# One PSUM bank moved from transposes to products in a two-layer decoder step, and output rows that begin in the heads' banks

## The chip, the cores and the metric

The kernel runs on one core of a Trainium2 chip. The metric is device time in microseconds (us), lower is better. The figures of before are the median of three runs and one execution taken by the hardware profiler. TensorE is called PE, VectorE DVE, ScalarE ACT, GpSimd POOL and SyncE SP, as in the profile.

## The reference

One inference step of a decoder trunk with two layers, for a prompt of 512 tokens and for 8 samples of 4 new tokens each, with the same weights. The change touches only the second layer (mixer B), from the attention over the shared latent cache to the final norm. Cut to that:

```
# MLA: q_lat, q_rope from a low-rank query; c_kv (256) and k_rope (64) shared by 8 heads
s = (einsum('bthc,bsc->bhts', q_lat, ckv) + einsum('bthr,bsr->bhts', q_rope, krope)) * MLA_SCALE
p = softmax(where(kpos <= qpos, s, -1e30))
o_lat = einsum('bhts,bsc->bthc', p, ckv)
tok = einsum('bthc,chd->bthd', o_lat, w_v_up)            # 8 heads x 128
mixed = concatenate([tok * silu(gate_t), mem_o * silu(gate_m)])   # 1024 + 512 wide
x = x + mixed @ w_out[l]                                  # 1536 x 1024
y = rmsnorm(x, g_final)
```

The prompt attends to its own 512 tokens. Each sample attends to 4096 cached tokens, which lie in 32 pages of 128 found through a page table, and to its own 4. `mem_o` is attention into 256 memory tokens. All data are float32.

## The kernel before, in words

Products that need float32 accuracy are made of three matmuls in a faster format: `split` (L88 to L91) makes a rounded high part (ACT, L89) and the remainder (L90, on DVE or on POOL, by its last argument), and `mm3` (L93 to L96) multiplies high by high, high by low and low by high. `transpose` (L135) is a matmul with the identity.

Up to about 478 us the kernel computes layer A, the shared keys and most gates. From L942 on the instruction order of PE and of SP (which issues most loads) is the order of the program text, while the other engines' instructions are ordered by the compiler's own scheduler. The program text is written by a planner: each piece of work is a generator (`Thread`, L947) that emits some instructions and then yields a pair, the PE time they are taken to need and the time until its next piece is due (both in us), or a condition. `weave` (L957) always continues the due thread that is least far along (`base + span * spent / work`). The planner knows nothing of PSUM banks, so a change of banks alone does not change the order.

The threads after 478 us:

- `round_scores` (rs) and `round_values` (rv): the samples' attention over the cache in 16 rounds. A round loads two halves of 8 pages (`load_half`, L998, into buffers `a` and `b`; a load is issued when the value matmuls of an earlier round have freed the buffer), transposes part of the keys (`turn_keys`, L1027; bank `tr`, copied out to `kt` by ACT L1019 or DVE L1021), multiplies queries by keys (L1051, L1060; bank `ac`), takes the softmax (L1069, L1071), transposes the weights (bank `tr`, copied out to `rt` by DVE L1083) and multiplies by the values (L1088; bank `ac`).
- `gates_late` (gl), then `head_inputs` (hi): queries, keys and values of the prompt's heads. Their products lie in bank `pa` and are read out by DVE L1227 (queries) or by a split (L89, L90 to `kx`, `vx`).
- `heads` (ha): per head, four blocks of scores (two banks `hs`), mask and softmax (L1280 to L1286, the last being the scaling of `e` by DVE), then per block transposes into `hs` (`turn_weights`), a split to `p`, and value products into bank `po`, read out by DVE L1320.
- `own_scores` (os_): the samples' scores against their own four tokens, in bank `tr`.
- `out_all` (out): the output projection in two column halves `fh` of 512. Each half has four row blocks of 128 tokens and six slabs of `w_out` (256 rows x 512 columns, tile `wr`, split into `wh` and `wl`). Slabs are made by `prepare` (L1359), three of them ahead of the output. Row blocks accumulate in four banks `oa` over all slabs; slab 4 is done together with slab 5, and `done` (L1400) adds the residual, sums squares and, in the second half, scales and stores.
- `sample_out` (so): `combine` puts the samples' partial attentions together through a chain of transposes and products in bank `tr`, and then six pairs of slabs (tile `ws`, five buffers, loaded again as PE frees them) give the samples' output rows in bank `ac` (L1622).

The order of the threads: rv, rs and gl until gl is done; rv, rs, ha and hi until all heads have their scores; rv, rs, ha and os_ until these are done; then the heads' banks are closed and four `oa` banks opened; at last so and out. The eight PSUM banks, each 128 x 512 float32, are shared out like this:

```
    rb = Banks(tr=2, ac=2)
    hb = Banks(pa=1, po=1, hs=2)
```

`ps_(tag)` gives the next bank of a tag; with one bank it waits for the last reader of the tile ahead.

Of the kernel before, what the change touches and what calls it, by code (L numbers as in the profile page):

```python
# [8 lines left out]
F32R = mybir.dt.float32r  # L9
# [6 lines left out]
P = 128  # L16
# [22 lines left out]
def trunk_kernel(ctx: ExitStack, tc: tile.TileContext, A, O):  # L39
    nc = tc.nc  # L40
# [47 lines left out]
    def split(h, l, src, eng=None):  # L88
        nc.scalar.copy(h, src)  # L89
        (eng or nc.vector).tensor_tensor(out=l, in0=src, in1=fr(h), op=ALU.subtract)  # L90
        return h, l  # L91
# [21 lines left out]
    ps_ = Banks(pa=4, tr=3, ac=1)  # L113
# [411 lines left out]
    t, v = load_w(wa[22], KD, P)  # L525
# [207 lines left out]
    for j in range(4):  # L733
        t = xo("o")
# [222 lines left out]
    def weave(threads, last):  # L957

        through = last if callable(last) else lambda: all(t.done for t in last)
        while not through():  # L960
            can = [
                t
                for t in threads
                if not t.done and t.at <= now[0] and (t.until is None or t.until())
            ]
            if not can:
                now[0] += 0.1
                assert now[0] < 2000
                continue
            t = min(can, key=Thread.behind)  # L970
            t.until = None
            got = next(t.gen, None)
            if got is None:
                t.done = True
            elif callable(got):
                t.until = got
            else:
                now[0] += got[0]
                t.spent += got[0]
                t.at = now[0] + got[1]  # L980


    rb = Banks(tr=2, ac=2)
    hb = Banks(pa=1, po=1, hs=2)

    def ps_(tag):
        return (rb if tag in rb.tags else hb)(tag)
# [361 lines left out]
    slabs = [(fh, s) for fh in range(2) for s in range(6)]  # L1349
    order = ([0, 1], [2, 3], [4, 5], [8, 9], [10, 11], [6, 7])  # L1350

    def slab(t, fh, s):
        k = order[s][0]
        v = t.rearrange("p (k c) -> p k c", k=2)
        src = wo[k * P : (k + 2) * P, fh * 512 : (fh + 1) * 512]
        nc.sync.dma_start(v, src.rearrange("(k p) c -> p k c", p=P))
        return v

    def prepare(fh, s):  # L1359
        if fh == 0:  # L1360
            for k in order[s]:
                mix_b(k)
        t = fin("wr")
        slab(t, fh, s)
        wh, wl = split(fin("wh", F32R), fin("wl", F32R), t, nc.gpsimd)
        return wh.rearrange("p (k c) -> p k c", k=2), wl.rearrange("p (k c) -> p k c", k=2)

    prepared = [prepare(*slabs.pop(0)) for _ in range(3)]
# [15 lines left out]
        gains_f.extend([gfin, gfs])  # L1384

    def out_rows(fh):
        pts = [ps_("oa") for _ in range(4)]

        pieces = [[(pts[j], 0, 512)] for j in (0, 3, 1, 2)]
        if fh:  # L1390
            pieces[3] = [(pts[2], 0, 256), (ps_("ac"), 256, 256)]

        def run(s, j, piece, wh, wl):
            ps, o, n = piece
            c, w = slice(j * P, (j + 1) * P), slice(o, o + n)
            for i, k in enumerate(order[s]):
                h, l = mixed[k]
                mm3(ps[:, :n], h[:, c], l[:, c], wh[:, i, w], wl[:, i, w], s == 0 and i == 0, s == 5 and i == 1)

        def done(j, p, ps, o, n):  # L1400
            f = slice(fh * 512 + o, fh * 512 + o + n)
            xf = x1n[j][:, f]
            nc.vector.tensor_tensor(out=xf, in0=ps[:, :n], in1=xf, op=ALU.add)
            c = 4 * j + 2 * fh + p
            nc.scalar.activation(pat("wu", n=n), xf, AF.Square, scale=D ** -0.5, accum_out=ssq[:, c : c + 1])
            if fh == 0:
                nc.vector.tensor_tensor(out=xf, in0=xf, in1=gains_f[0][:, f], op=ALU.mult)
                return
            if p < len(pieces[j]) - 1:
                return  # L1410
            sm = st(3)
            others = [4 * j] + [4 * j + 2 + i for i in range(p)]
            so_far = EPS
            for i, o_ in enumerate(others):
                nc.vector.tensor_scalar(
                    out=sm[:, i : i + 1], in0=ssq[:, o_ : o_ + 1], scalar1=so_far, scalar2=None, op0=ALU.add
                )
                so_far = sm[:, i : i + 1]
            r = st(1)
            nc.vector.tensor_scalar(  # L1420
                out=sm[:, 2:3], in0=ssq[:, c : c + 1], scalar1=so_far, scalar2=None, op0=ALU.add
            )
            nc.gpsimd.tensor_tensor(out=r, in0=sm[:, 2:3], in1=mhalf[:, :1], op=ALU.pow)
            nc.scalar.activation(x1n[j][:, :512], x1n[j][:, :512], AF.Copy, scale=r)
            nc.sync.dma_start(O["y_p"][0, j * P : (j + 1) * P, :512], x1n[j][:, :512])
            xf = x1n[j][:, 512:]
            nc.vector.scalar_tensor_tensor(out=xf, in0=xf, scalar=r, in1=gains_f[0][:, 512:], op0=ALU.mult, op1=ALU.mult)
            nc.sync.dma_start(O["y_p"][0, j * P : (j + 1) * P, 512:], xf)

        late = []  # L1430
        for s in range(6):
            wh, wl = prepared.pop(0)
            late.append((s, wh, wl))
            if s == 4:
                continue
            for j in range(4):
                for p, piece in enumerate(pieces[j]):
                    for one in late:
                        run(one[0], j, piece, *one[1:])
                        yield 1.4 / len(pieces[j]), 0.0  # L1440
                    if s == 5:
                        if not x1n:
                            yield lambda: x1n
                        done(j, p, *piece)
            for _ in late:
                if slabs:
                    prepared.append(prepare(*slabs.pop(0)))
            late = []

    def out_all():  # L1450
        yield from out_rows(0)
        yield from out_rows(1)
# [29 lines left out]
        yield 0.5, 0.0  # L1482

    os_ = Thread(own_scores(), 1.0, 0.0, 1.0, now[0])
    weave([rv, rs, ha, os_], [ha, os_])
    hb.close()
    hb = Banks(oa=4)
    out = Thread(out_all(), 112 / total, 66 / total, 66.0, now[0])
    weave([rv, rs, out], [rv, rs])
    sp_order.__exit__(None, None, None)  # L1490
    nats.close()
# [113 lines left out]
    def sample_out():  # L1605
        todo = [(fh, s) for fh in range(2) for s in range(6)]
        o = cb("o").rearrange("p (b c) -> p b c", b=NB - 1)
        nc.sync.dma_start(o, ostore.rearrange("b p c -> p b c"))
        parts.update({b: o[:, b, :] for b in range(NB - 1)})
        v = [pat("vx") for k in range(2)]  # L1610
        for k in range(2):
            src = A["w_v_up"][k * P : (k + 1) * P].rearrange("p h c -> p (h c)")
            nc.sync.dma_start(v[k], src)
        here = [slab(cb("ws"), *todo.pop(0)) for _ in range(5)]
        yield from combine(cb, v)
        for fh in range(2):
            psm = ps_("ac")
            for s, ks in enumerate(order):
                v = here.pop(0)
                for i, k in enumerate(ks):  # L1620
                    for j in range(4):
                        nc.tensor.matmul(  # L1622
                            psm[j * NS : (j + 1) * NS, :P],
                            lhsT=gs[:, k, :],
                            rhs=v[:, i, j * P : (j + 1) * P],
                            start=s == 0 and i == 0,
                            stop=s == 5 and i == 1,
                        )
                if todo:
                    here.append(slab(cb("ws"), *todo.pop(0)))  # L1630
                if s % 2:
                    yield 0.88, 0.5
            fs = slice(fh * P, (fh + 1) * P)
            nc.vector.tensor_tensor(out=x1s[:, fs], in0=psm[:, :P], in1=x1s[:, fs], op=ALU.add)
            nc.scalar.activation(pat("wu")[:, :P], x1s[:, fs], AF.Square, accum_out=sss[:, fh : fh + 1])
        sq = st(1)
        nc.vector.tensor_tensor(out=sq, in0=sss[:, 0:1], in1=sss[:, 1:2], op=ALU.add)
        yield 0.0, 1.5
        po = ps_("tr")
        nc.tensor.matmul(po[:, 0:1], lhsT=jsum, rhs=sq, start=True, stop=True)  # L1640
        r = rstd_cols(po[:, 0:1], 1, P, D)
        nc.vector.scalar_tensor_tensor(out=x1s, in0=x1s, scalar=r, in1=gains_f[1], op0=ALU.mult, op1=ALU.mult)
        for j in range(4):
            nc.sync.dma_start(
                O["y_s"].rearrange("b t (f j c) -> j (b t) f c", f=2, j=4)[j],
                x1s[j * NS : (j + 1) * NS, :].rearrange("p (f c) -> p f c", f=2),
            )
# [134 lines left out]
```

## Time and profile before

| | us |
|---|---|
| median of 3 runs | 840.11 |
| lowest and highest run | 835.95, 843.13 |
| the profiled execution | 836.81 |
| its span, first to last instruction | 835.0 |
| PE busy in that span | 782.3 (94%) |
| DVE busy | 495.0 (59%) |
| ACT busy | 316.1 (38%) |
| POOL busy | 242.3 (29%) |

Busy times overlap between engines. A line of the profile names source line, engine, operation and tiles as out<-in without buffer numbers. A value in brackets behind an instruction is the idle time of its engine just ahead of it and what ended it. A table of stretches gives for each engine the busy time and in brackets the number of instructions. PE's clock is the share of full speed that was granted.

### The profile page before, as it was taken

The numbers are of one execution on the slowest core, as the hardware profiler recorded it, in microseconds if no ns is written. First come the engines' busy times: TensorE is split into PE (matmuls) and PEld (weight loads), VectorE is DVE, ScalarE is ACT, GpSimd is POOL, SyncE is SP. The second block draws the span as 40 slices with busy tenths as digits, with TensorE's granted clock in tenths as the row PEclk, the third lists the DMA queues.
The fourth block names the chain that finished last, engine by engine and source line by source line (L and its number), as shares of the span: only waits on it lengthen the run. The fifth ranks groups of instructions, "written<-read, shape, count | busy, mean of one in ns | idle before, by whom it ended". The sixth has DMA issues, their size and how long they took to land.

```text
span 835.0 us, 17362 instructions
## 1 busy us (share of the span) xinstructions
PE 782.3 (94%) x6814; PEld 669.6 (80%) x6814; DVE 495.0 (59%) x942; ACT 316.1 (38%) x631; POOL 242.3 (29%) x216
## 2 busy tenths in 40 slices
PE   6999999999999999889999999897999899979895
PEld 6989998999999989768998886675676667757584
DVE  6757666798834435965676545565566474673213
ACT  7453333432433234435343223434344443522212
POOL 0035220111243323404332435352142141054141
PEclk9999999999999999999999999999999999989998
DMA  8356247431233337347426698897897887778512
GB/s 308 93 182 222 75 177 263 148 89 52 77 95 95 85 118 222 123 137 237 164 69 248 217 388 310 316 360 255 312 362 260 299 322 270 249 271 291 204 55 101
DMA packets 83060, 169.54 MB, mean 203 GB/s; under 512 B 9377, under 2 KB 26402, under 8 KB 82722
## 3 DMA queue, kind: packets, MB, share of 16 engines
q1 hardware_dynamic: 77170, 149.61, 52.5%
q0 software_dynamic: 5808, 18.82, 6.1%
q8 instruction: 54, 0.88, 0.4%
q14 instruction: 28, 0.23, 0.1%
HBM read 157.19 MB, written 11.21 MB: 202 GB/s over the span
## 4 chain that ended last, share of the span: by engine, by line
PE 72%; DMA 10%; DVE 9%; ACT 4%; issue 2%; SPq 1%; POOL 1%; POOLq 0%; DVEq 0%; ACTq 0%
PE pa L94 15%; PE pa L96 14%; PE pa L95 14%; DMA b<-in_cache_P 4%; PE tr L135 4%; PE ac L1088 3%; PE ac L1051 3%; PE oa L94 2%; PE oa L96 2%; PE oa L95 2%; DMA ws<-in_w_out_b 2%; PE ac L1060 1%; PE ac L393 1%; DMA wr<-in_w_mem_v 1%; SPq L1010 1%
## 5 line engine op out<-in xcount | busy, mean ns | idle before, releaser
L94 PE MATMUL pa<-h,wh 128*128 128x272 f32 x832 | 239.1, 290 | 0.0
L96 PE MATMUL pa<-h,wl 128*128 128x272 f32 x832 | 236.0, 289 | 1.1 <-POOL wl L90 1.1
L90 POOL TENSOR_TENSOR wl<-wr,wh 128x1024 fp32r<-128x1024 f32 (+1 forms) x57 | 129.6, 2275 | 203.3 <-ACT wh L89 182.7
L95 PE MATMUL pa<-h,wh 128*128 128x272 f32 x640 | 183.6, 288 | 0.0
L94 PEld LDWEIGHTS pa<-h,wh 128*128 128x128 f32 x832 | 156.2, 188 | 4.9 <-issue 3.9
L96 PEld LDWEIGHTS pa<-h,wl 128*128 128x128 f32 x832 | 154.9, 188 | 2.7 <-POOL wl L90 1.6
L89 ACT CAST wh<-wr 128x1024 fp32r<-128x1024 f32 (+1 forms) x87 | 87.7, 1008 | 178.7 <-PE pa L95 68.7
L95 PEld LDWEIGHTS pa<-h,wh 128*128 128x128 f32 x640 | 120.2, 188 | 1.0
L95 PE MATMUL pa<-g,wh 128*128 128x272 f32 x192 | 54.6, 288 | 0.8 <-DVE g L90 0.8
L90 DVE TENSOR_TENSOR wl<-wr,wh 128x1024 fp32r<-128x1024 f32 x30 | 36.7, 1223 | 15.6 <-ACT wh L89 15.5
L265 DVE SCALAR_TENSOR_TENSOR g<-t,g 128x272 f32<-128x272 f32 x40 | 36.0, 908 | 7.1 <-ACT t L264 7.1
L264 ACT ACTIVATE t<-g 128x272 f32<-128x272 f32 x40 | 16.6, 427 | 57.2 <-DVE g L251 57.2
L94 PE MATMUL oa<-wh,c 128*128 128x512 f32 (+1 forms) x96 | 38.0, 395 | 0.0
L1284 ACT ACTIVATE e<-hs,s 128x128 f32<-128x128 f32 (+3 forms) x32 | 16.9, 527 | 53.0 <-DVE s L1282 53.0
L95 PEld LDWEIGHTS pa<-g,wh 128*128 128x128 f32 x192 | 36.1, 188 | 1.0 <-DVE g L90 1.0
L95 PE MATMUL oa<-wl,c 128*128 128x512 f32 (+1 forms) x96 | 36.4, 380 | 0.0
L1051 PE MATMUL ac<-kt,c 128*32 128x256 f32 x128 | 33.5, 384 | 2.9 <-ACT kt L1019 1.5
L1051 PE MATMUL ac<-a,c 128*32 128x256 f32 x384 | 35.4, 386 | 0.0
L1088 PE MATMUL ac<-a,rt 128*32 128x256 f32 x384 | 32.5, 393 | 0.1
L1088 PE MATMUL ac<-b,rt 128*32 128x256 f32 x128 | 32.3, 393 | 0.0
L251 DVE SCALAR_TENSOR_TENSOR g<-pa,r 128x272 f32<-128x272 f32 x38 | 16.3, 437 | 21.8 <-PE pa L96 21.7
L135 PE MATMUL tr<-c,b 128*128 128x128 f32 x128 | 21.2, 280 | 6.5 <-DMA b<-in_cache_P 6.1
(411 smaller groups left out, 1804.9 us busy)
## 6 DMA issues: line engine op xcount, KB each, us to landing
a<-in_cache_P SPq DMA_DIRECT2D x192, 288.0 KB, 5.5
wr<-in_w_in_a SPq DMA_DIRECT2D x24, 512.0 KB, 3.9
b<-in_cache_P SPq DMA_DIRECT2D x64, 160.0 KB, 5.8
wr<-in_w_in_b SPq DMA_DIRECT2D x19, 512.0 KB, 4.0
cs<-in_mem_kT SPq DMA_DIRECT2D x16, 512.0 KB, 5.4
wr<-in_w_out_a SPq DMA_DIRECT2D x16, 384.0 KB, 3.1
wr<-in_w_out_b SPq DMA_DIRECT2D x12, 512.0 KB, 5.2
ws<-in_w_out_b SPq DMA_DIRECT2D x12, 512.0 KB, 7.6
```

Of the source, the lines that this page charges most:

```text
L89: nc.scalar.copy(h, src)
L90: (eng or nc.vector).tensor_tensor(out=l, in0=src, in1=fr(h), op=ALU.subtract)
L94: nc.tensor.matmul(out, lhsT=wh, rhs=xh, start=start, stop=False)
L95: nc.tensor.matmul(out, lhsT=wh, rhs=xl, start=False, stop=False)
L96: nc.tensor.matmul(out, lhsT=wl, rhs=xh, start=False, stop=stop)
L135: nc.tensor.transpose(out, in_, ident[:k, :k])
L251: nc.vector.scalar_tensor_tensor(out=out[:, o : o + HALF], in0=ps[:, :HALF], scalar=scale, in1=bc[:, o : o + HALF], op0=ALU.mult, op1=ALU. ...
L264: nc.scalar.activation(th[:, :HALF], z[:, o : o + HALF], AF.Tanh)
L265: nc.vector.scalar_tensor_tensor(out=z[:, o : o + HALF], in0=th[:, :HALF], scalar=1.0, in1=z[:, o : o + HALF], op0=ALU.add, op1=ALU.mult,)
L1051: nc.tensor.matmul(o[j * NS : (j + 1) * NS, :], lhsT=QT[:, k, b, :], rhs=nat[ih][0][:, 2 * j : 2 * j + 2, c] if j < 3 else kt[ih][:, k], s ...
L1088: nc.tensor.matmul(po[j * NS : (j + 1) * NS, :256], lhsT=pT[:, i * P + j * NS : i * P + (j + 1) * NS], rhs=nat[i // 2][j // 3][:, 2 * j % ...
L1284: nc.scalar.activation(e, ps[:, :n], AF.Exp, bias=nx, accum_out=sm)
```

## The change

Four things change.

- `tr` has one bank instead of two, `pa` two instead of one.
- The output thread is made before the heads are done and woven with them from 12 us (of the planner's time) after the last scores. Its first row block lies in a `pa` bank and takes the first three slabs before it waits for the heads' end (`ha.done`). Then row blocks 1 and 2 take the two `hs` banks and row block 3 takes `po`. In the second half row block 3 lies half in `po` and half in `ac`. The heads' banks stay open to the end; there are no `oa` banks.
- The first three slabs are loaded through POOL's DMA queue instead of SP's, and the subtraction of their split is on DVE instead of POOL.
- Each pair of the samples' output slabs is due 3.0 us after the last one ended, instead of 0.5.

```diff
--- before.py
+++ after.py
@@ -980,8 +980,8 @@
                 t.at = now[0] + got[1]
 
 
-    rb = Banks(tr=2, ac=2)
-    hb = Banks(pa=1, po=1, hs=2)
+    rb = Banks(tr=1, ac=2)
+    hb = Banks(pa=2, po=1, hs=2)
 
     def ps_(tag):
         return (rb if tag in rb.tags else hb)(tag)
@@ -1349,11 +1349,11 @@
     slabs = [(fh, s) for fh in range(2) for s in range(6)]
     order = ([0, 1], [2, 3], [4, 5], [8, 9], [10, 11], [6, 7])
 
-    def slab(t, fh, s):
+    def slab(t, fh, s, queue=None):
         k = order[s][0]
         v = t.rearrange("p (k c) -> p k c", k=2)
         src = wo[k * P : (k + 2) * P, fh * 512 : (fh + 1) * 512]
-        nc.sync.dma_start(v, src.rearrange("(k p) c -> p k c", p=P))
+        (queue or nc.sync).dma_start(v, src.rearrange("(k p) c -> p k c", p=P))
         return v
 
     def prepare(fh, s):
@@ -1361,8 +1361,8 @@
             for k in order[s]:
                 mix_b(k)
         t = fin("wr")
-        slab(t, fh, s)
-        wh, wl = split(fin("wh", F32R), fin("wl", F32R), t, nc.gpsimd)
+        slab(t, fh, s, nc.gpsimd if (fh, s) < (0, 3) else None)
+        wh, wl = split(fin("wh", F32R), fin("wl", F32R), t, nc.vector if (fh, s) < (0, 3) else nc.gpsimd)
         return wh.rearrange("p (k c) -> p k c", k=2), wl.rearrange("p (k c) -> p k c", k=2)
 
     prepared = [prepare(*slabs.pop(0)) for _ in range(3)]
@@ -1384,11 +1384,8 @@
         gains_f.extend([gfin, gfs])
 
     def out_rows(fh):
-        pts = [ps_("oa") for _ in range(4)]
-
-        pieces = [[(pts[j], 0, 512)] for j in (0, 3, 1, 2)]
-        if fh:
-            pieces[3] = [(pts[2], 0, 256), (ps_("ac"), 256, 256)]
+
+        pieces = [[(ps_("pa"), 0, 512)]]
 
         def run(s, j, piece, wh, wl):
             ps, o, n = piece
@@ -1428,12 +1425,20 @@
             nc.sync.dma_start(O["y_p"][0, j * P : (j + 1) * P, 512:], xf)
 
         late = []
+        if fh == 0:
+
+            for s in range(3):
+                run(s, 0, pieces[0][0], *prepared[s])
+                yield 1.4, 0.0
+            yield lambda: ha.done
+        pieces += [[(ps_("hs"), 0, 512)], [(ps_("hs"), 0, 512)]]
+        pieces += [[(ps_("po"), 0, 256), (ps_("ac"), 256, 256)] if fh else [(ps_("po"), 0, 512)]]
         for s in range(6):
             wh, wl = prepared.pop(0)
             late.append((s, wh, wl))
             if s == 4:
                 continue
-            for j in range(4):
+            for j in range(fh == 0 and s < 3, 4):
                 for p, piece in enumerate(pieces[j]):
                     for one in late:
                         run(one[0], j, piece, *one[1:])
@@ -1482,10 +1487,8 @@
         yield 0.5, 0.0
 
     os_ = Thread(own_scores(), 1.0, 0.0, 1.0, now[0])
-    weave([rv, rs, ha, os_], [ha, os_])
-    hb.close()
-    hb = Banks(oa=4)
-    out = Thread(out_all(), 112 / total, 66 / total, 66.0, now[0])
+    out = Thread(out_all(), 112 / total, 66 / total, 66.0, now[0] + 12.0)
+    weave([rv, rs, ha, os_, out], [ha, os_])
     weave([rv, rs, out], [rv, rs])
     sp_order.__exit__(None, None, None)
     nats.close()
@@ -1629,7 +1632,7 @@
                 if todo:
                     here.append(slab(cb("ws"), *todo.pop(0)))
                 if s % 2:
-                    yield 0.88, 0.5
+                    yield 0.88, 3.0
             fs = slice(fh * P, (fh + 1) * P)
             nc.vector.tensor_tensor(out=x1s[:, fs], in0=psm[:, :P], in1=x1s[:, fs], op=ALU.add)
             nc.scalar.activation(pat("wu")[:, :P], x1s[:, fs], AF.Square, accum_out=sss[:, fh : fh + 1])
```

## The prediction

> **What bounds the kernel now.** I read the page first, then a table of stretches, then the waits of TensorE, and last single instructions where the diff touches them.
>
> ```profile
> span 835.0 us, 17362 instructions
> PE 782.3 (94%) x6814; PEld 669.6 (80%) x6814; DVE 495.0 (59%) x942; ACT 316.1 (38%) x631; POOL 242.3 (29%) x216
> ```
>
> TensorE (PE) is busy for 782.3 of 835.0 us, and its order is written out by hand. What the change can win or lose is therefore PE's idle time, and it touches nothing ahead of 478 us. The stretches, in the column order PE, PEld, DVE, ACT, POOL, then PE clock, DMA share and GB/s:
>
> ```profile
> 478.00:730.00 252.00, 232.07 (x2486) 173.09 (x2485) 145.55 (x321) 99.96 (x238) 76.77 (x82) 1.00 0.87 307
> 730.00:742.00 12.00, 7.55 (x60) 4.45 (x57) 10.59 (x22) 5.11 (x11) 9.33 (x8) 0.72 0.55 176
> 742.00:774.00 32.00, 32.00 (x223) 23.52 (x223) 13.18 (x34) 7.10 (x10) 13.73 (x11) 1.00 0.84 308
> 774.00:790.00 16.00, 13.26 (x190) 8.83 (x189) 3.75 (x6) 3.12 (x9) 0.80 (x1) 1.00 0.75 264
> 790.00:824.00 34.00, 34.00 (x184) 28.77 (x177) 8.25 (x16) 8.52 (x15) 12.87 (x8) 1.00 0.16 51
> ```
>
> PE idles 252.00 − 232.07 = 19.9 us while heads and cache rounds are woven together, 12.00 − 7.55 = 4.45 us in the last head, and 2.7 us among the sample rows. The other two stretches are full. Who ended the idle time, from 478 to 742 us (total, times, longest):
>
> ```profile
> PE tr L135 <- DMA b<-in_cache_P: 6.1, 6, 2.4
> PE pa L94 <- DVE t L1227: 4.5, 5, 1.8
> PE hs L135 <- DVE e L1286: 4.5, 1, 4.5
> PE pa L94 <- DVE kx L90: 1.4, 1, 1.4
> PE pa L94 <- DVE c L1106: 1.3, 1, 1.3
> PE pa L94 <- DVE vx L90: 0.6, 1, 0.6
> ```
>
> The four `pa` rows are matmuls that wait until the one `pa` bank has been read out: 4.5 + 1.4 + 1.3 + 0.6 = 7.8 us. (The row with `c L1106` names the DVE instruction that came last; the read-out of `vx` stands just ahead of it.)
>
> **Part 1: two `pa` banks, one `tr` bank.** PE's order does not change here: the planner counts costs and due times, not banks. With a second bank the 7.8 us go. The first stall is not won:
>
> ```profile
> 516.59 0.50 PE L94 MATMUL pa<-c,qh 128*128 128x512 f32 x1 [1.82 <-DVE t L1227]
> 526.97 0.30 PE L135 MATMUL tr<-c,b 128*128 128x128 f32 x1 [2.40 <-DMA b<-in_cache_P]
> ```
>
> Ten us after the stall of 1.82 PE waits 2.40 for a cache load, so an earlier PE waits longer there. Of the other 6.0 us I keep 4.8: loads are issued when PE frees a buffer, so most of them move with PE, but the other load waits of the 6.1 stay, and what is late next after a freed `pa` group is often a `kt` copy. The bounds are 0 (every stall comes back as a load wait) and 7.8.
>
> One `tr` bank costs whenever a transposing set begins before the set ahead of it has been copied out. Going through the 48 sets of this stage (128 + 64 transposes, four to a set), I find few that lie so close:
>
> ```profile
> L135 PE MATMUL tr<-c,b x128: 270/273/330, 488.5 to 724.0; 128*128 128x128 f32 x128
> L135 PE MATMUL tr<-c,rt x64: 270/272/331, 506.3 to 729.8; 128*128 128x128 f32 x64
> ```
> ```profile
> 595.02 0.60 PE L135 MATMUL tr<-c,rt 128*128 128x128 f32 x4
> 595.22 0.69 DVE L1021 COPY kt<-tr 128x512 f32<-128x512 f32 x1 [0.71 <-PE tr L135]
> 534.71 0.60 PE L135 MATMUL tr<-c,rt 128*128 128x128 f32 x4
> 535.42 0.57 ACT L1019 COPY kt<-tr 128x512 f32<-128x512 f32 x1
> 550.36 0.69 DVE L1083 COPY rt<-tr 128x512 f32<-128x512 f32 x1
> 551.07 0.60 PE L135 MATMUL tr<-c,b 128*128 128x128 f32 x4
> ```
>
> At 595.02 the set would start at 595.22 + 0.69 = 595.91, 0.9 us later. At 534.71 it would wait until 535.99; what follows waits for that same copy, so only the set's own time of some 0.5 us is added. At 551.07 it is 0.1 us; three more places look like this one and get 0.1 each. That is −1.8 us. Behind each waiting set stand all later matmuls, of heads and rounds alike, since PE runs in order. The bounds: 0, if the copies come earlier than now, and 16 × (0.69 + 0.5) = 19 us, if the one value set of each of the 16 rounds came right behind a key set. I take the low end, since the order of sets stays as traced. Heads stage: 7.8 − 1.8 − 1.2 − 1.8 = **+3.0 us**.
>
> **Part 2: row 0 in the heads' banks, three splits moved to DVE, their loads to POOL's queue.**
>
> ```profile
> 731.33 2.33 POOL L90 TENSOR_TENSOR wl<-wr,wh 128x1024 fp32r<-128x1024 f32 x1 [17.41 <-DMA wr<-in_w_out_b]
> 731.53 2.15 DVE L1108 TENSOR_TENSOR s<-c,s 128x1 f32<-128x1 f32 x1
> 734.38 0.47 DVE L1286 TENSOR_SCALAR e<-e,s 128x512 f32<-128x512 f32 x1
> 734.90 0.47 PE L135 MATMUL hs<-c,e 128*128 128x128 f32 x1 [4.45 <-DVE e L1286]
> 735.10 2.32 DVE L1113 SCALAR_TENSOR_TENSOR c<-s,s,c 128x1 f32<-128x1 f32 x1
> L90 DVE TENSOR_TENSOR wl<-wr,wh 128x1024 fp32r<-128x1024 f32 x30 | 36.7, 1223 | 15.6 <-ACT wh L89 15.5
> ```
>
> PE's largest gap, 4.45 us, ends when the last softmax scale (L1286) is done. Ahead of it a one-column DVE instruction took 2.15 us; it ends at 733.68, with POOL's split (733.66). A second took 2.32. DVE was held while POOL worked. [...] With the splits on DVE both holds go, some 2.0 us each; in return DVE gets three instructions of 1.22 us. The gap shortens by 2.0 if none of them comes ahead of L1286, by 0.8 if one does, and grows by 1.7 if three do. I take 1.5, near the first: L1108 is stuck behind the first split as it begins, and the other two slabs land later.
>
> [...] The nearest row for an issue on POOL:
>
> ```profile
> 712.18 0.54 POOL L1342 DMA_DIRECT2D tab<-gmd  x1 [2.51 <-DVE t L90]
> ```
>
> Three issues at 0.54 lie in POOL's idle 17.41 us above, and a load that waits for its buffer there holds up no POOL work of the stage. I cost them at nothing; without that cover, 1.6.
>
> The clock fell after the gap:
>
> ```profile
> 734.00:736.00 2.00, 1.10 (x9) 0.58 (x13) 2.00 (x6) 1.58 (x4) 1.00 (x1) 0.50 0.46 141
> 735.37 3.01 PE ac L1088 x32
> 721.80 1.86 PE ac L1088 x32
> 743.54 0.23 PE oa L96
> ```
>
> The granted clock was 0.50, and 32 value matmuls took 3.01 us instead of 1.86: 1.15 us. Between 478 and 730 idle times of up to 2.4 us left it at 1.00. The new gap, about 3.0, lies between 2.4 and 4.45; I count 0.7 of the 1.15. [...]
>
> Row 0 on three slabs is 18 matmuls at 0.23 = 4.1 us. It does not fill the 4.45 us gap. Following the planner, `out` becomes available 12 us after the last scores, while the head's third transposing set falls due, by the yields, at 5.0 + 0.44 + 1.0 (until the value halves are due) + 2 × 0.86 + 0.33 + 1.2 + 0.70 + 0.3 = 10.7. So row 0 stands between that set and the second value product, behind the gap in PE's order. There it hides only some 0.5 us of waiting for `p`. Its matmuls are moved, not saved. Stage: 1.5 + 0.7 + 0.5 = **+2.7 us** (bounds −1.7 and 2.0 + 1.15 + 0.5 = 3.7).
>
> **Part 3: what lies behind it.** From 742 to 774 PE is full, but slabs 4 and 5 come in late:
>
> ```profile
> wr<-in_w_out_b SPq DMA_DIRECT2D x4, 512.0 KB, 19.8
> SPq L1608 <- PE ac L1088: 4.1, 1, 4.1
> ```
>
> Between 738 and 766 us they land 19.8 us after issue, behind other loads. The burst starts when PE ends its last value matmuls (second row), so it moves with PE. PE itself comes earlier by perhaps 0.5 us more than the burst: **−0.5**.
>
> **Part 4: sample rows 3.0 apart.**
>
> ```profile
> PE ac L1622 <- DMA ws<-in_w_out_b: 2.7, 4, 1.1
> 774.33 7.32 DMA ws<-in_w_out_b
> ```
>
> PE waits 2.7 us for sample slabs, which need 7.3 us to land once PE frees a buffer. A pair of steps now spans 0.88 + 3.0 = 3.9 us instead of 1.4, so five buffers go round in 2.5 × 3.9 = 9.7 us, more than 7.3. I count **+2.3**; the bounds are 0 and 2.7. Six pairs end by 773 + 23 = 796, covered by the full stretch to 824.
>
> The sum: 3.0 + 2.7 − 0.5 + 2.3 = 7.5 us. The profiled execution takes 836.81 us (span 835.0 and 1.8 around it); it would take 829.3. The median of the runs, 840.11, lies 3.3 above that execution; against it I forecast 832.6.
>
> **The rivals.** *Only the end is won.* The freed `pa` stalls come back as load waits (6.1 us of them are there already, and the DMA share is 0.87), and the single `tr` bank costs 1.8: 2.7 − 0.5 + 2.3 − 1.8 = 2.7 us, 837.4. Against it: only one `pa` stall has a load wait closely behind it.
>
> *The gap closes.* DVE reaches the last scale 2.0 us earlier, the clock never falls, all `pa` stalls but the first stay won: 6.0 − 1.8 + 3.7 + 2.7 = 10.6 us, 829.5. For it: both holds stand in the rows.
>
> *The single `tr` bank stalls PE (slower).* Place: cache rounds, 478 to 730. Once PE no longer stops at `pa`, it meets transposing sets before ACT and DVE have copied the last one. Each costs 0.69 + 0.5 = 1.2 us; 7.5 + 1.8 = 9.3 us of stalls cancel the forecast, which is 8 of the 48 sets; at 14 of them the kernel loses 7.5: 847.6. Against it: the order is the same, and most sets lie farther from the copy ahead of them than the pairs shown.
>
> **How the numbers follow.** Forecast 0.50 (830 to 836), only the end 0.20, gap closes 0.17, `tr` stalls 0.13. Faster by over 1% means under 831.7, which is about what a measurement tells from no change: all of the third case, and half of the forecast's own spread: 0.17 + 0.25 = 0.42. Slower by over 1% is over 848.5, half of the last case and a little for a mis-sized end: 0.09. The rest is 0.49. The range 825.5 to 841 takes in the first three cases, 4 us below the lowest of them because the runs of before themselves reach 4.2 us below their median, and leaves out most of the fourth.
>
> **What would show it.** The waits of `pa` on L1227 and L90 gone and those of `tr` on its copies below 3 us (part 1). [...] No wait for `ws` over 0.5 us (part 4). I am wrong if new `tr` waits pass 5 us, if load waits grow by what `pa` loses, or if DVE's splits stand ahead of L1286.

## The result, and the profile after

The changed kernel takes 830.74 us (median of four runs, 830.10 to 831.33). The kernel before takes 838.84 us in the same comparison (four runs, 835.95 to 843.13). The ratio is 0.9899, with a 95% interval from 0.987 to 0.9929: about 1% faster, 8.1 us between the medians. The profiled execution takes 830.1 us, 6.7 less than the 836.81 of before.

The first lines of the page of the changed kernel:

```profile
span 828.3 us, 17376 instructions
PE 784.7 (95%) x6814; PEld 672.7 (81%) x6814; DVE 489.5 (59%) x945; ACT 315.5 (38%) x631; POOL 237.3 (29%) x216
```

PE is busy about as long as before (784.7 against 782.3 us), so the span lost idle time of PE, nothing else. DVE is busy for 5.5 us less although it took over three subtractions of 1.2 us: it is held less, as the rows of the last head show below. The stretches of the changed kernel (column order as in the prediction), moved forward by as much as the work moved:

```profile
478.00:722.00 244.00, 227.18 (x2391) 169.38 (x2389) 140.60 (x310) 96.81 (x232) 77.48 (x83) 0.99 0.89 316
722.00:734.00 12.00, 10.15 (x132) 6.41 (x130) 10.10 (x27) 6.66 (x13) 2.01 (x3) 0.82 0.44 138
734.00:766.00 32.00, 32.00 (x174) 23.77 (x171) 13.04 (x31) 7.73 (x12) 12.82 (x14) 0.96 0.91 327
766.00:782.00 16.00, 16.00 (x152) 12.21 (x151) 7.02 (x17) 4.83 (x10) 5.55 (x3) 1.00 0.36 123
```

PE now idles 16.8 us while heads and cache rounds are woven (19.9 before), 1.85 us in the last head (4.45 before), and not at all in the sample rows (2.7 before). But its clock is 0.99 instead of 1.00 in the first of these stretches: a part of the busy time there is slow work. What PE waited for in the changed kernel from 478 to 727 us (total, times, longest):

```profile
PE tr L135 <- DMA b<-in_cache_P: 5.4, 6, 2.3
PE tr L135 <- ACT rt L1071: 2.5, 2, 1.4
PE tr L135 <- ACT kt L1019: 2.3, 2, 1.4
PE tr L135 <- DVE rt L1083: 2.1, 1, 2.1
PE ac L1051 <- DVE kt L1021: 1.7, 2, 1.5
PE ac L1051 <- ACT kt L1019: 1.4, 2, 0.7
PE tr L135 <- ACT e L1284: 0.9, 1, 0.9
PE po L100 <- ACT p L89: 0.2, 1, 0.2
```

No wait of `pa` is left. New are the waits of `tr` on `kt` L1019, `rt` L1083 and `e` L1284, 2.3 + 2.1 + 0.9 = 5.3 us. The load waits (first row) are 5.4 where they were 6.1, so they did not take back what `pa` gave up.

To say where the 6.7 us lie, PE's order gives three marks: the first key transpose, the last score matmul (L1279) and the last value matmul (L102). The groups of the changed kernel, with the times of the first and the last start behind the durations:

```profile
L135 PE MATMUL tr<-c,b x128: 270/273/474, 488.0 to 721.9; 128*128 128x128 f32 x128
L1279 PE MATMUL hs<-c,qr x32: 272/308/401, 531.9 to 725.5; 128*128 128x128 f32 x8, 128*128 128x256 f32 x8, 128*128 128x384 f32 x8, 128*128 128x512 f32 x8
L102 PE MATMUL po<-p,vx x32: 273/334/628, 551.7 to 742.0; 128*128 128x512 f32 x8, 128*128 128x384 f32 x8, 128*128 128x256 f32 x8, 128*128 128x128 f32 x8
```

The last two of the kernel before:

```profile
L1279 PE MATMUL hs<-c,qr x32: 274/306/401, 530.9 to 727.5; 128*128 128x128 f32 x8, 128*128 128x256 f32 x8, 128*128 128x384 f32 x8, 128*128 128x512 f32 x8
L102 PE MATMUL po<-p,vx x32: 273/338/442, 550.6 to 741.3; 128*128 128x512 f32 x8, 128*128 128x384 f32 x8, 128*128 128x256 f32 x8, 128*128 128x128 f32 x8
```

| stretch | before, us | after, us | gain | forecast |
|---|---|---|---|---|
| start to first key transpose | 488.5 | 488.0 | 0.5 | 0 |
| heads stage, to the last score | 239.0 | 237.5 | 1.5 | 3.0 |
| last head, to the last value product, without row 0 (4.1) | 13.8 | 12.4 | 1.4 | 2.7 |
| from there to the end, with row 0 | 93.7 | 90.4 | 3.3 | 1.8 (−0.5 + 2.3) |

The total is close to the forecast's, and two of its terms came out at half their size in this pair of executions. The traces of the experiments below say that much of this is the scatter of a single pair.

### The profile page after: what moved, and what is told of

It is laid out like the page before. It is cut to its first block, busy times and chain, and to the rows that moved or that the text cites. A ratio compares the mean times of both kernels' runs of the same rounds, so it can differ in the third digit from the quotient of the medians.

```text
span 828.3 us, 17376 instructions
## 1 busy us (share of the span) xinstructions
PE 784.7 (95%) x6814; PEld 672.7 (81%) x6814; DVE 489.5 (59%) x945; ACT 315.5 (38%) x631; POOL 237.3 (29%) x216
## 4 chain that ended last, share of the span: by engine, by line
PE 74%; DVE 9%; DMA 8%; ACT 4%; issue 2%; SPq 1%; POOL 1%; POOLq 0%; DVEq 0%; ACTq 0%
PE pa L94 15%; PE pa L96 15%; PE pa L95 15%; DMA b<-in_cache_P 5%; PE tr L135 4%; PE ac L1088 3%; PE ac L1051 3%; PE hs L94 2%; PE hs L95 2%; PE hs L96 2%; PE ac L1060 1%; PE ac L393 1%; SPq L1010 1%; DMA wr<-in_w_mem_v 1%; PE hs L135 1%
## 5 line engine op out<-in xcount | busy, mean ns | idle before, releaser
L90 POOL TENSOR_TENSOR wl<-wr,wh 128x1024 fp32r<-128x1024 f32 (+1 forms) x54 | 122.1, 2263 | 185.6 <-ACT wh L89 182.4
L90 DVE TENSOR_TENSOR wl<-wr,wh 128x1024 fp32r<-128x1024 f32 x33 | 40.3, 1220 | 15.5 <-ACT wh L89 15.4
L1284 ACT ACTIVATE e<-hs,s 128x128 f32<-128x128 f32 (+3 forms) x32 | 16.9, 528 | 51.7 <-DVE s L1282 51.7
L1088 PE MATMUL ac<-a,rt 128*32 128x256 f32 x384 | 34.2, 408 | 0.2
L1088 PEld LDWEIGHTS ac<-a,rt 128*32 128x32 f32 x384 | 14.9, 116 | 13.9 <-issue 5.7
L95 PE MATMUL pa<-wl,mh 128*128 128x512 f32 x64 | 25.2, 402 | 1.1 <-DVE wl L90 1.1
```

The lines of the kernel that those rows point to most:

```text
L95: nc.tensor.matmul(out, lhsT=wh, rhs=xl, start=False, stop=False)
L1088: nc.tensor.matmul(po[j * NS : (j + 1) * NS, :256], lhsT=pT[:, i * P + j * NS : i * P + (j + 1) * NS], rhs=nat[i // 2][j // 3][:, 2 * j % ...
L1284: nc.scalar.activation(e, ps[:, :n], AF.Exp, bias=nx, accum_out=sm)
```

## The experiments

**The banks alone, and the single `tr` bank alone.** In the kernel before:

```diff
-    rb = Banks(tr=2, ac=2)
-    hb = Banks(pa=1, po=1, hs=2)
+    rb = Banks(tr=1, ac=2)
+    hb = Banks(pa=2, po=1, hs=2)
```

The second run makes only the first of these edits and leaves `hb` as it was:

```diff
-    rb = Banks(tr=2, ac=2)
+    rb = Banks(tr=1, ac=2)
```

> The kernel before with nothing but one tr bank and two pa banks. Theory (banks are worth about 2 us: the last head's scores ended 2.05 us earlier in the changed kernel): 2 us faster than before, pa waits 7.8 -> 0, new tr waits of about 5 us. Rival (the banks only trade one wait for another, the start of the stage drifted by 0.5 us anyway): within 0.5 us of before. My recorded term of 3.0 us would be right if it comes out 2.5 us or more faster.

> The kernel before with one tr bank and one pa bank (seven banks in use). It prices the single tr bank by itself. Theory: the places where a transposing set lies close behind a copy cost 2 to 4 us, so 2 to 4 us slower than before. Recorded working: 1.8 us slower. Rival (the slower case of the prediction): 9 us or more slower.

Measured: with both bank changes the ratio to before is 0.9947 [0.9921, 0.9974], with the single `tr` bank alone 1.0028 [1.0007, 1.0049]. The heads stage takes 236.5 and 242.3 us. PE's waits with both bank changes, from 478 us on:

```profile
PE tr L135 <- DMA b<-in_cache_P: 6.7, 7, 2.1
...
PE tr L135 <- DVE rt L1083: 2.1, 1, 2.1
PE tr L135 <- ACT kt L1019: 1.9, 2, 1.0
```

And with the single `tr` bank alone:

```profile
PE pa L94 <- DVE t L1227: 4.7, 5, 1.8
...
PE tr L135 <- ACT kt L1019: 1.0, 1, 1.0
PE tr L135 <- DVE s L1285: 0.9, 1, 0.9
```

So the banks are a gain of their own, 4.4 us of the run by the ratio (2.2 to 6.6 by its interval). The long `tr` wait of 2.1 us on `rt` is there only when `pa` has two banks. It is the same late DVE as before, met one step further on: the prediction shows a `pa` stall of 1.82 us at 516.59, and this is what stands in its place in the changed kernel's timeline:

```profile
518.98 0.66 PE L135 MATMUL tr<-c,b 128*128 128x128 f32 x4 [2.07 <-DVE rt L1083]
```

A matmul into `pa` waited there for DVE's read-out of the queries; now the next transposing set waits for DVE's copy of the set ahead, which stands in the same queue (it starts at 518.23, behind two copies, L768, of 2.04 us; at 518.66 in the kernel before, where a second `tr` bank was free).

**The banks undone in the changed kernel.**

```diff
-    rb = Banks(tr=1, ac=2)
-    hb = Banks(pa=2, po=1, hs=2)
+    rb = Banks(tr=2, ac=2)
+    hb = Banks(pa=1, po=1, hs=2)
```

> The changed kernel with two tr banks and one pa bank again; woven row 0, DVE splits, POOL loads and spacing stay. Theory: the parts add up, so it is about 2 us slower than the changed kernel and about 6 us faster than before; pa waits of about 7.8 us are back. Rival (the second pa bank matters mainly for the output rows): the pa waits before the last head's scores differ little, and new pa waits stand in the output rows, over 1 us.

Measured: 0.9954 [0.993, 0.9978], so about half of the gain is lost. The waits of `pa` are back, and the stage takes 240.5 us. Over all traces the stage takes 239.0, 239.4, 240.5 and 239.5 us with two `tr` banks and one `pa` bank (mean 239.6, four kernels) and 235.3 to 238.9 us with one and two (mean 236.7, nine kernels). By these means the banks are worth 2.9 us in this stage. One trace lies up to 2.2 us from the mean of its group, so a single pair, such as the 1.5 us of the table above, does not measure it.

**The spacing alone.** In the kernel before:

```diff
-                    yield 0.88, 0.5
+                    yield 0.88, 3.0
```

> The kernel before with only the samples' slab pairs 3.0 us apart. Theory: the 2.7 us of ws waits go and nothing takes their place: 2.5 to 2.8 us faster than before, and four oa banks as before. Rival: the later sample rows push something behind them, less than 1 us faster.

Measured: 0.9956 [0.9933, 0.9979], that is 3.7 us of 838.84; the wait for `ws` is gone from PE's list. In the traces the stretch behind the last value product is 90.3 us long instead of 93.7: the waits of 2.7 us are gone, and PE's busy time there is 0.6 us shorter as well (80.97 against 81.58), for which no run shows the reason.

**DVE's subtractions alone.** In the kernel before:

```diff
-        wh, wl = split(fin("wh", F32R), fin("wl", F32R), t, nc.gpsimd)
+        wh, wl = split(fin("wh", F32R), fin("wl", F32R), t, nc.vector if (fh, s) < (0, 3) else nc.gpsimd)
```

> The kernel before with only the first three subtractions on DVE; banks, order of TensorE, loads and spacing stay. Theory (DVE was held by POOL's subtractions): no one-column DVE instruction over 1 us near the last head, the wait for the last softmax scale falls from 4.45 us to about 2.5, the products behind it no longer wait for p, about 2 us faster than before. Rival (DVE's own 3.7 us take the place of the holds): the wait stays over 4 us and the time within 0.7 us of before.

Measured: 0.9977 [0.9958, 0.9997], that is 1.9 us. From the last score to the last value product PE needs 1.8 us less than before, the wait for L1286 is 2.4 us instead of 4.5, and no one-column instruction of DVE is held there.

**The reverse: the changed kernel with these subtractions on POOL.**

```diff
-        wh, wl = split(fin("wh", F32R), fin("wl", F32R), t, nc.vector if (fh, s) < (0, 3) else nc.gpsimd)
+        wh, wl = split(fin("wh", F32R), fin("wl", F32R), t, nc.gpsimd)
```

> The changed kernel with the first three slabs' subtractions on POOL again (loads stay on POOL's queue). Theory (DVE is held while POOL subtracts): one-column DVE instructions of over 2 us are back near the last head, the wait for the last softmax scale is again 3.5 us or more instead of 1.0, and the kernel is about 2 us slower than the changed one (about 6 us faster than before). Rival (the gap became shorter for another reason, such as the order of DVE's work): the wait stays under 1.5 us and the time within 0.7 us of the changed kernel.

Measured: 0.9978 [0.9954, 1.0002], so the kernel is some 6.6 us slower than the changed one, where about 2 were expected. The wait for L1286 stays at 1.0 us, since POOL's first split came behind it this time. But DVE is held all the same, and others wait for it. DVE in this kernel, then POOL, then PE's waits:

```profile
729.33 2.01 DVE L1112 TENSOR_TENSOR c<-s,s 128x1 f32<-128x1 f32 x1
731.26 2.54 DVE L1114 TENSOR_SCALAR os<-os,s 128x256 f32<-128x256 f32 x1
```
```profile
728.96 7.04 POOL L90 TENSOR_TENSOR wl<-wr,wh 128x1024 fp32r<-128x1024 f32 x3 [2.37 <-DMA wr<-in_w_out_b]
```
```profile
PE po L102 <- DVE p L90: 3.1, 1, 3.1
...
PE pa L96 <- DVE t L90: 1.9, 1, 1.9
```

While POOL makes three splits in 7.0 us, DVE needs 2.0 us for an operation on one column and 2.5 for one that takes 0.33 in the changed kernel, and the value products wait 3.1 us for `p`. So the move to DVE is needed; only the victim changes with the order. The 1.9 us are at 769, in the second half of the output, where POOL makes the split in the changed kernel too: there DVE's two subtractions of `t` start with POOL's split (766.45 and 766.38) and take 3.45 us, while in the changed kernel they stand ahead of it and take 1.28.

**The loads on SP's queue.**

```diff
-        slab(t, fh, s, nc.gpsimd if (fh, s) < (0, 3) else None)
+        slab(t, fh, s)
```

> The changed kernel with the first three slabs loaded through SP's queue again. Theory (the queue does not matter, the loads wait for their buffers): within 0.7 us of the changed kernel. Rival (on SP they hold up the loads behind them): 1 us or more slower, with slab loads and sample loads landing later.

Measured: 0.9888 [0.984, 0.9937], the same as the change (0.9899) as far as four runs can tell, whose interval is some 4 us to either side. The traces are closer: from the last score to the end they need 102.5 us on SP's queue and 102.8 on POOL's. No effect of the queue shows here, in either direction.

**Row 0: not woven in, and woven in earlier.** In the changed kernel:

```diff
-    out = Thread(out_all(), 112 / total, 66 / total, 66.0, now[0] + 12.0)
-    weave([rv, rs, ha, os_, out], [ha, os_])
+    weave([rv, rs, ha, os_], [ha, os_])
+    out = Thread(out_all(), 112 / total, 66 / total, 66.0, now[0])
```

> The changed kernel with the output thread started only when the heads are done, in the same banks. Theory (row 0 hides only the wait for the last weights' splits, about 0.5 us, its matmuls are moved and not saved): 0.3 to 1 us slower than the changed kernel. Rival (weaving row 0 is where the end gained): 3 us or more slower.

```diff
-    out = Thread(out_all(), 112 / total, 66 / total, 66.0, now[0] + 12.0)
+    out = Thread(out_all(), 112 / total, 66 / total, 66.0, now[0] + 3.0)
```

> The changed kernel with the output thread due 3 us after the last scores instead of 12, so that two slabs of row 0 stand in PE's order ahead of the last head's first transposing set and the third right behind it. Theory (row 0 as it is placed fills little of the gap): if the first slab is split in time, the wait for the last softmax scale is filled and the clock stays up, 1 to 3 us faster than the changed kernel. Rival (the slab's split is late): PE waits for the split instead, 1 to 4 us slower, and this shows why 12 was needed.

Measured: not woven in, 0.992 [0.9891, 0.9949], which is the change's ratio within the intervals. The last head takes 12.1 us against 12.4 of the change without row 0. So row 0 hides nothing that shows where the planner puts it; the half microsecond of the forecast is less than these runs can resolve. Woven in 9 us earlier it costs most of the gain, 0.9991 [0.9969, 1.0014]. PE's waits in that kernel:

```profile
PE pa L96 <- DVE p L90: 3.2, 1, 3.2
...
PE pa L95 <- DVE wl L90: 1.5, 1, 1.5
PE pa L94 <- ACT wh L89: 1.4, 1, 1.4
```

PE meets row 0 at 729.4 us, before its slabs are split, and stands 1.4 + 1.5 us in front of them. The 3.2 us are at 769.9, in the second half of the output rows, where the changed kernel has no wait. DVE is late there because it is held again: its two subtractions of `p` start at 767.02, with a split that POOL makes in every one of these kernels (766.95, 2.34 us), and take 3.42 us; in the changed kernel the same two stand ahead of POOL's split and take 1.28. With the 0.97 us of the changed kernel's gap set against them, these 6.1 us are 5.1 of the 6.3 by which the span is longer.

**The samples' own scores 12 us later.** The clock still fell in the last head of the changed kernel (as it does in all 14 traces, for 3.4 or 6.8 us), and this run moves away the last thing that lies ahead of the fall, 48 matmuls with 32 columns of weights and 4 moving columns each.

```diff
-    os_ = Thread(own_scores(), 1.0, 0.0, 1.0, now[0])
+    os_ = Thread(own_scores(), 1.0, 0.0, 1.0, now[0] + 12.0)
```

> The changed kernel with the samples' 48 small own-score products 12 us later in the planner's time, behind row 0. In both kernels they stand in the 2 us ahead of the fall of the clock to 0.50, which lasts 6.5 us though the waits behind them are 0.75 and 0.97 us. Theory (the small products count as idle time for the clock): without them there the clock stays at 1.00 or falls later, the 32 value matmuls take about 1.9 us instead of 3.6, about 1 us faster in all, since the 1.6 us of small products are no longer hidden in the gap. Rival (the waits alone lower the clock): it falls as now, and the kernel is 1.5 us slower.

Measured: 0.9941 [0.9912, 0.9969], no gain on the change (0.9899) and rather a loss, though the intervals overlap. With nothing between the scores and it, the wait for L1286 is 3.0 us, and the clock is low for 3.4 us behind it instead of 6.8. But it falls once more at 744.27, 3 us behind the small matmuls at their new place. The stretches of this kernel:

```profile
740.00:744.00 4.00, 3.10 (x52) 2.56 (x50) 2.82 (x9) 0.23 (x1) 1.13 (x2) 1.00 1.03 380
744.00:748.00 4.00, 4.00 (x12) 3.08 (x12) 2.01 (x6) 0.34 (x1) 0.00 (x0) 0.57 1.06 354
```

PE waits for 0.9 us in the first row and not at all in the second, whose clock is 0.57. So here the clock fell at a wait of 3.0 us without the small matmuls. The cause of the second fall is mixed: in the 3.41 us ahead of it lie the last 0.5 us of the small matmuls, the wait of 0.9 us and the narrow transposes of `combine`, and this run does not tell them apart.

**The small matmuls by themselves.** The changed kernel with the own scores' products made four more times (192 matmuls, into the free `tr` bank, read by nobody), far from any wait, in the second half of the output rows:

```diff
+            if fh == 1 and s == 1:
+                tiny = ps_("tr")[:NS, :NS].rearrange("p (b t) -> p b t", b=NB)
+                for _ in range(4):
+                    for b in range(NB):
...
```

> The changed kernel with the samples' own-score products emitted four more times (192 small matmuls, about 6.5 us, into a spare use of the tr bank that nobody reads) in the middle of the second half's output rows, where TensorE waits for nothing. It measures what the clock makes of them. Theory (small products count as idle): the granted clock falls to 0.50 during or right behind them, and the output matmuls that follow take up to twice as long for 3.4 or 6.8 us; the span grows by 8 to 10 us. Rival (only waits count): the clock stays at 1.00 and the span grows by 6.5 us.

Measured in one execution: 837.54 us, 7.4 above the change's profiled execution. PE has no wait there, and most of the 7.4 are the small matmuls' own time: 48 of them take some 1.65 us in the changed kernel at full clock, so 192 take 6.6. By the time alone, 7.4 lies between the two cases; the clock decides. Three stretches of it, the first two within the small matmuls, the third behind them:

```profile
786.00:788.00 2.00, 2.00 (x69) 2.00 (x67) 0.00 (x0) 0.13 (x1) 1.80 (x1) 1.00 0.96 363
790.00:792.00 2.00, 2.00 (x41) 2.00 (x41) 0.00 (x0) 0.00 (x0) 0.00 (x0) 0.50 0.00 0
796.00:798.00 2.00, 2.00 (x38) 1.34 (x36) 0.00 (x0) 0.00 (x0) 0.00 (x0) 1.00 0.00 0
```

PE is busy without a break, 2.00 of 2.00 us in each row, and the granted clock falls to 0.50 all the same. So much is shown: in this execution 192 matmuls with 32 columns of weights and four moving columns did not hold the clock up.

**Three edits alone.** The kernel before with the banks, the three DVE subtractions and the spacing, its output rows still in `oa` banks behind the heads and its loads on SP's queue (the three diffs above, put together).

> The kernel before with three of the change's edits: one tr and two pa banks, the first three subtractions on DVE, sample rows 3.0 us apart. Output rows still begin behind the heads, in four oa banks, and all slab loads go through SP's queue. Theory (these three hold all of the gain, woven row 0 and POOL's queue none): ratio 0.988 to 0.993, as the changed kernel (0.990). Rival (the heads' banks and the woven row carry part of it): 0.994 or more. Sum of the parts measured alone: -4.4, -3.7 and -1.9 us would give 0.988.

Measured: 0.993 [0.991, 0.995], a span of 828.1 us against 828.3 of the change. The intervals of the two ratios overlap. By the ratios these three edits carry 0.7% of the 1.0%. By the spans they carry all of it, but the traced execution is the fastest of its six, 3.9 us below their median. What the rest of the change is worth stays open: the ratios put it at 2.6 us, give or take 3. Each alone, the three gave 4.4, 1.9 and 3.7 us (one minus the ratio, times 838.84), 10.0 in all, each to within some 2; the whole change, by the same reckoning, gives 8.5.

## Why the prediction was right or wrong

**The forecast as a whole held:** 832.6 was forecast and 830.74 measured; the sum was 7.5 us, the traced pair shows 6.7 and the medians 8.1. Part of that is luck. The two large terms were each made of wrong sizes that cancel, one of them with a step that failed, and the two small ones were off by 0.5 and 1.1 us.

**Heads stage, +3.0: right, its parts not.** The means of the traces differ by 2.9. But one `tr` bank costs 242.3 − 239.6 = 2.7 us instead of 1.8 (by one trace; the ratio of its runs gives 2.3), and the second `pa` bank wins 242.3 − 236.7 = 5.6 instead of 4.8. What the single bank loses was counted from the places where two sets lie close in the trace of before. The stall that goes to the next user of the same late engine was not in that count: the first `pa` stall came back in full as a `tr` wait of 2.07 us. The prediction did take 1.8 us off for that stall, the right size for a wrong reason: the load wait ten us later, which was to grow by it, is 2.27 us instead of 2.40. My own mark, new `tr` waits above 5 us, was passed (5.3), and it was a bad mark: a wait that only takes the place of another adds no time.

**The traced pair shows 1.5, in part because of the clock.** It fell behind two load waits in the changed kernel, and nowhere in this stage before. That this makes the difference is argued, not shown: load waits differ between the traces as well. The two stretches of the changed kernel, then those of the kernel before:

```profile
528.00:532.00 4.00, 4.00 (x41) 3.02 (x40) 1.11 (x2) 0.00 (x0) 3.17 (x4) 0.57 1.05 382
583.00:586.00 3.00, 3.00 (x24) 1.52 (x28) 0.00 (x0) 0.58 (x1) 0.00 (x0) 0.50 1.04 403
```
```profile
528.00:532.00 4.00, 4.00 (x54) 3.58 (x53) 2.17 (x5) 0.75 (x3) 2.51 (x3) 1.00 1.06 386
583.00:586.00 3.00, 3.00 (x51) 1.74 (x47) 0.48 (x1) 0.00 (x1) 0.56 (x1) 1.00 1.07 402
```

PE is full in all four, with half as many matmuls in the second row as in the fourth.

**Last head, +2.7: the step that failed is the clock.** "I take 1.5" for the shorter gap was too careful. DVE in the changed kernel:

```profile
728.80 0.13 DVE L1108 TENSOR_TENSOR s<-c,s 128x1 f32<-128x1 f32 x1
729.63 0.47 DVE L1286 TENSOR_SCALAR e<-e,s 128x512 f32<-128x512 f32 x1
730.96 1.21 DVE L90 TENSOR_TENSOR wl<-wr,wh 128x1024 fp32r<-128x1024 f32 x1
732.19 0.20 DVE L1113 SCALAR_TENSOR_TENSOR c<-s,s,c 128x1 f32<-128x1 f32 x1
```

L1108 takes 0.13 us instead of 2.15 and L1113 0.20 instead of 2.32, and the first split stands behind L1286. PE's waits in the last head of the changed kernel:

```profile
PE hs L135 <- DVE e L1286: 1.0, 1, 1.0
PE tr L135 <- ACT e L1284: 0.8, 1, 0.8
```

The last transpose of the head's first block waits 0.97 us instead of 4.45, and the cache round's set ahead of it waits 0.75. (The profile names `e`, which ended last. I take it for a wait until the own scores have been read out of the one `tr` bank: it stands in every trace with one `tr` bank in which the own scores lie there, and in none with two.) That is 2.7 us of waiting less. The gap itself has two causes: the wait for L1286 is 4.5 us before, 2.4 with the DVE subtractions alone, 3.1 with the banks alone and 1.0 with both. But the next step, that a gap between 2.4 and 4.45 us leaves most of the clock (0.7 of 1.15 us), is false: the clock won nothing. The chain of waits of the changed kernel has

```profile
730.78 3.62 PE ac L1088 x32
```

where before had 3.01 and a full clock gives 1.86. With a gap of a quarter the length (0.97 us against 4.45), the clock was 0.50 for as long, 6.83 us in both traces. A finer cut of the kernel before shows why, and I could have made it: the row with 0.50 that I quoted tells that the clock was low, not when it fell. In steps of 3.41 us, half of those 6.83, the kernel before:

```profile
727.44:730.85 3.41, 3.01 (x58) 2.38 (x56) 3.37 (x10) 2.15 (x5) 0.00 (x0) 1.00 0.44 134
730.85:734.26 3.41, 0.00 (x0) 0.00 (x0) 3.41 (x6) 0.82 (x3) 2.33 (x1) 0.50 0.48 178
```

and the changed kernel:

```profile
726.32:729.73 3.41, 2.12 (x44) 1.82 (x41) 3.41 (x12) 1.52 (x5) 2.01 (x3) 1.00 0.53 145
729.73:733.14 3.41, 2.86 (x25) 1.37 (x29) 3.41 (x8) 2.43 (x5) 0.00 (x0) 0.50 0.88 310
733.14:736.55 3.41, 3.41 (x20) 2.02 (x13) 3.07 (x5) 1.20 (x2) 1.74 (x4) 0.50 0.72 246
```

Before, the gap begins at 734.90 − 4.45 = 730.45, and the clock falls 0.4 us into it: the gap as a whole cannot be what lowered it. In the 3.41 us ahead of the fall PE counts as 88% busy (3.01 of 3.41), more than half of it with the small matmuls; without them 43% are left. That the clock answers to this stretch, and that the gap only kept it down for the second 3.41 us, is my inference; the counts in the last section fit it. (The prediction has the clock fall after the gap and looks for a length between 2.4 and 4.45 us that a gap must reach. The trace does not agree: the clock fell 0.4 us into the gap.)

The size, again, is luck in part. The pair shows 1.4 us, but over the traces this stretch takes 14.4 us with the first splits on POOL (13.8 to 14.8, five kernels) and 12.2 with them on DVE (12.0 to 12.4, seven kernels; row 0 taken off as above, and without the two kernels whose order differs there). That is 2.2 us, which is the forecast's 1.5 + 0.7 with both sizes wrong: the moved subtractions shorten the gap by 2.1, and the clock adds nothing.

**Row 0, +0.5: not seen.** The last head is no shorter with it than in the run without the weaving, and the times of the two do not differ beyond their intervals. The order was off by a step as well: row 0 stands behind the fourth transposing set, ahead of the third value product, as PE shows in the changed kernel:

```profile
737.18 0.27 PE L135 MATMUL hs<-c,e 128*128 128x128 f32 x1
737.21 0.47 PE L94 MATMUL pa<-wh,c 128*128 128x512 f32 x1
...
741.48 0.28 PE L100 MATMUL po<-p,vx 128*128 128x256 f32 x1
```

**The moved loads, 0:** nothing speaks against it; on SP's queue the time is the same within the interval. **The late slabs, −0.5:** did not come; PE is full from 734 to 766. **The sample rows, +2.3:** mis-sized, 3.4 by the trace of the spacing alone (93.7 to 90.3), above their bound of 2.7. All of the waiting went, and 0.6 us of PE's busy time with it. Put together, 2.9 + 2.2 + 3.4 make 8.5 us, what the ratio of the whole change gives.

**The rivals.** *Only the end is won* is out: load waits did not grow in the traced pair, and the banks alone are a gain. *The gap closes* was right on the gap and wrong on the clock, and its time, 829.5, is closer to the measured one than the forecast, through terms that missed to both sides. *The single `tr` bank stalls PE* has its mechanism (2.7 us for the single bank) but not its size: it needed 9.3.

## What to carry to other kernels

A wait that is taken from an engine whose order is written out can come back at the next instruction that depends on the same late producer (here 1.82 us at `pa` as 2.07 us at `tr`), so count producers, not stalls. When PE's clock is low behind a gap, look at the few microseconds ahead of the fall before blaming the gap: tiny matmuls that look 100% busy can be part of the cause (while 192 of them ran, PE busy without a break, the clock fell to 0.50 here), and closing the gap then need not bring the clock back (from 4.45 to 0.97 us here, with 6.83 us at 0.50 in both). Try a large edit as its single parts: here three one-line edits (how banks are shared, which engine subtracts, how far apart the steps are due) hold some two thirds of the gain or more, and the woven first row could not be shown to add anything.

## What the runs showed of the hardware that was not expected

In each trace the granted clock changes only at times that lie whole multiples of 3.413 us apart, and every low stretch between 480 us and the end of the output rows lasts a multiple of it: from 730.85 us on for 6.827 us in the kernel before, in the changed one from 528.34 and from 582.95 for 3.413 each and from 729.72 for 6.827. I cut the 14 traces, from 480 us on, into these windows and added up the moving columns of the matmuls that end in each (a matmul of 512 columns starts every 0.23 us at full clock, so a full window holds some 7,600). Of 1,334 windows at full clock, all 17 with fewer than 2,300 columns were followed by half clock, of the 87 with 2,300 to 4,300 only 12, and of the rest none. The window ahead of the fall in the changed kernel held about 1,040. So in these traces the fall goes with how much PE streamed in one such window, and not with the length of a wait alone; the window of before begins at 727.44, its gap at 730.45. A wait of 2.40 us at 527 us left the clock alone in the kernel before, where it lay across two windows (1.5 and 0.9 us); behind one of 2.27 us at the same place it fell to 0.50 in the changed one, with 1.75 us in one window. Columns are not the only measure that fits. The 32-column matmuls of the cache rounds start four at a time (within 0.03 us at 731.18 in the changed kernel, the next four 0.43 us later, at a clock of 0.50) and count four times here. By PE's busy time without the four-column matmuls the windows part more sharply: all 23 that were busy for less than 0.445 of their length fell, of the 63 up to 0.63 only 6, and above that none. These bounds are read off the same windows and no run tested them; what decides between them, and whether a low stretch lasts one window or two, is open. The clock may also make part of the scatter between executions, since by an estimate a window at a clock of 0.50 costs up to 1.7 us (half of its 3.41).

DVE was held beside POOL's split not only in operations of a tensor with a tensor (L1108, 2.15 us in the kernel before and 0.13 in the changed one). L1114, an operation of a tensor with one scalar per row, took 2.54 us beside the splits on POOL and 0.33 in the changed kernel, where POOL makes no split between 726 and 743 us; this is one row of one trace.
